# S1 of Strassen's scheme by accumulating transfers from DRAM instead of an addition on DVE

## The chip, the cores and the metric

The kernel runs on one core of a Trainium2 chip. The metric is the device time of one execution, in microseconds (us). The kernel before took 2231.31, 2233.18 and 2235.49 us in three runs, a median of 2233.18 us. The engines are called as in the profile: PE does matmuls (PEld is its loading of weights), DVE, ACT and POOL work on vectors, SP issues transfers. POOL's instruction stream can issue transfers too.

## The reference, cut to what matters

Two layers of a decoder trunk; x is 512 tokens by 1024 features, all in float32. A layer is a half-step feed-forward block, a mixer with three groups of attention heads, a cross-attention into 256 memory tokens, and a second half-step feed-forward block, each behind a layer norm. The change touches the feed-forward blocks, of which there are four in all:

```python
def swiglu(x, w_in, w_out):
    a, b = jnp.split(x @ w_in, 2, axis=-1)
    return (jax.nn.silu(a) * b) @ w_out

x = layer_norm(ALPHA * x + 0.5 * swiglu(x, ffn1_w_in[l], ffn1_w_out[l]), ln_g[l, 0], ln_b[l, 0])
```

`w_in` is 1024 x 5632 (the two halves a and b of 2816 columns each), `w_out` is 2816 x 1024. It also touches a small table of the mixer: the sliding-window attention adds a bias per head and distance, looked up in `rel_bias` (32 buckets, 8 heads).

## The kernel before, in words

**Precision.** Every float32 matrix product is done as three matmuls on rounded parts: a value is split into a high part H (a cast, on ACT) and a low part L = value - H (a subtraction, on DVE), and H·H, H·L and L·H are accumulated in PSUM (`mm3`, L201). `prep` (L256) splits a weight block that has landed in a buffer `raw` into `wH` (ACT) and `wL` (DVE). Each has four buffers, so that the preparation can run up to four blocks ahead of PE. The activations are held transposed and split as `xTH` and `xTL`.

**A feed-forward block** (`Ffn`, L522) has eleven pairs q of column blocks of 256, for a and for b. The first two pairs (q = 0 and 1, the plain part, with f = 0 to 3) are ordinary products. For q = 2 to 10 one round of Strassen's scheme (in Winograd's form) is used: the 1024 rows of the weights are halved (a1, a2 for the half a; b1, b2 for the half b), the 512 tokens too (B11 to B22), and seven products of 24 matmuls of 256 columns take the place of eight. The right-hand sides T1 to T4, sums of the quarters of x, are formed once for each block in `combine` (L279) from `xr` = H + L; two of these four additions run on POOL, two on DVE. The left-hand sides are formed for each q: S1 = b1 + b2, S2 = S1 - a1, S3 = a1 - b1, S4 = a2 - S2, all in float32 on DVE, 128 x 1024 elements each, each followed by its own split into wH and wL. S1 and S2 share one buffer `sw`; S3 is written over b1, S4 over a2. The order of the seven products of a round in the program (L688 to L734) is: a1·B11, S1·T1, S2·T2, then b2·T4 of the round before, a2·B21, S4·B22 of the round before, and S3·T3.

**Weights.** `load` (L560) brings a1 and b1 as two transfers of 512 KB into one `raw` buffer, a2 and b2 into another. There are three `raw` buffers, so a1, b1 of the next round go into the buffer that S4 (in a2's place) of the round before frees, and a2, b2 of the next round into the one that S3 (in b1's place) of this round frees. All transfers are issued by SP, in one order.

**What sets the order.** The program is written as straight code; a scheduler of the framework then orders the instructions of each engine by its own estimate of when their operands are ready, and every engine runs its instructions strictly in that order. A wait at the head of an engine's queue holds everything behind it. A rough clock in the kernel (L33) decides when side work (`tick`) is put in between.

**Side work in the first block.** `swa_bias` (L463) builds the bias table of the mixer during the first feed-forward block: for each of eight heads a matmul, a fill of a tile F by POOL, a copy by DVE, and two transfers over DRAM. F has one buffer of its own. The tag `scr` (four buffers) serves the Strassen rounds as u2 and u3, among other uses.

Of the kernel before, what the change touches and what calls it, by code (L numbers as in the profile page):

```python
# [7 lines left out]
F32 = mybir.dt.float32  # L8
F32R = mybir.dt.float32r
AF = mybir.ActivationFunctionType  # L10
ALU = mybir.AluOpType

P = 128
# [9 lines left out]
SWH = 8  # L23
# [4 lines left out]
NB = 32  # L28
# [114 lines left out]
class Net:  # L143
# [215 lines left out]
    def out_proj(self, nk, act, wsrc, scale, l, lni, nxt, tail=4, drain_at=0, done=None):  # L359
# [4 lines left out]
        for c in range(2):  # L364
# [9 lines left out]
            body = gr[:len(gr) - ntail]  # L374

            cut = drain_at if c == 0 and drain_at else len(body)
            for gi, (k0, n) in enumerate(body[:cut]):
                if c == 0 and gi == 0 and not drain_at:
# [84 lines left out]
    def swa_bias(self):  # L463
        nc, A, c = self.nc, self.A, self.const
        self.biasT = c.tile([P, SWH, 2 * P], F32, name="biasT")
        with self.tc.tile_pool(name="biasp", bufs=1) as bp, \
                self.tc.tile_pool(name="biasd", bufs=1, space=bass.MemoryType.DRAM) as dp:
            hot = bp.tile([NB, P], F32, name="hot")
            nc.sync.dma_start(hot, A["bucket_hot"])
            rb = bp.tile([NB, SWH], F32, name="rb")  # L470
            nc.sync.dma_start(rb, A["rel_bias"])
            for h in range(SWH):
                yield 4.0
                b = self.bank()
                nc.tensor.matmul(b[:, :P], rb[:, h:h + 1].broadcast_to([NB, P]), hot, start=True, stop=True)
                F = bp.tile([P, 383], F32, tag="F", name=self.nm("F"), bufs=1)
                nc.gpsimd.memset(F, -1e30)
                nc.vector.tensor_copy(F[:, P:2 * P], b[:, :P])
                d = dp.tile([P * 383], F32, tag="biasD", name=self.nm("biasD"), bufs=SWH)
                nc.sync.dma_start(d.rearrange("(p n) -> p n", n=383), F)  # L480
                nc.sync.dma_start(self.biasT[:, h],
                                  d[127:127 + P * 382].rearrange("(p n) -> p n", n=382)[:, :2 * P])
# [39 lines left out]
class Ffn:  # L522
# [17 lines left out]
    def open(self):  # L540
        n = self.net
        self.ctx, self.inner = ExitStack(), ExitStack()
        self.fp = self.ctx.enter_context(n.tc.tile_pool(name=n.nm("ffn"), bufs=1))
        self.h = {}
        self.ip = self.inner.enter_context(n.tc.tile_pool(name=n.nm("ffnin"), bufs=1))
        self.p1 = [self.ip.tile([P, S], F32, name=n.nm("p1")) for _ in range(2)]
        self.sw = self.ip.tile([P, 4, 256], F32, name=n.nm("sw"))
        self.T = [[self.ip.tile([P, 4, self.HT], F32R, name=n.nm("T")) for _ in range(2)] for _ in range(4)]

    def block(self, q, part, half):  # L550
# [101 lines left out]
    def body(self, nxt):  # L652
        n, nc = self.net, self.net.nc
        V, ACT = nc.vector, nc.scalar
        prev = None

        def rest(r):

            q, Y, b2 = r["q"], r["Y"], r["b2"]
            self.product(Y, b2, "T4", False)  # L660
            V.tensor_mul(self.hid(q, 0), self.hid(q, 0), self.pair(Y))

        def last(r):

            q, W, u2, u3 = r["q"], r["W"], r["u2"], r["u3"]
            self.product(W, r["s4"], "B22", False)
            V.tensor_add(u2, W, u2)
            ACT.activation(self.hid(q, 1), self.pair(u2), AF.Silu)
            V.tensor_mul(self.hid(q, 1), self.hid(q, 1), self.pair(u3))

        self.open()
        for f in range(2 * self.PLAIN):
            q = f // 2
            if f % 2 == 0:
                self.h[q] = self.two("h")
            h = self.h[q][:, f % 2]
            bs = []
            for part in range(2):
                if f < 2:
                    W, b = self.first[2 * f + part]  # L680
                    n.proj_T(b, W, 256, 512)
                else:
                    W, b = self.cols(f, part), n.bank()
                    n.proj_T(b, W, 0, S)
                bs.append(b)
            ACT.activation(h, bs[0], AF.Silu)
            V.tensor_mul(h, h, bs[1])
            if f == 0:  # L688
                self.combine()
        for q in range(self.PLAIN, self.Q):  # L690
            a1, b1 = self.load(q, 0)
            a2, b2 = self.load(q, 1)
            s = self.sw
            V.tensor_add(s, b1, b2)
            p1, X = self.p1[q % 2], n.bank()
            self.product(X, a1, "B11", True)
            ACT.copy(p1, X)
            W, Y = n.bank(), n.bank()
            self.product(W, s, "T1", True)
            V.tensor_sub(b1, a1, b1)  # L700
            V.tensor_sub(s, s, a1)
            self.product(Y, s, "T2", True)
            V.tensor_add(Y, Y, p1)
            u2 = n.scr()
            ACT.copy(u2, Y)
            if prev:
                rest(prev)
            def p2():
                self.product(X, a2, "B21", False)
                self.gate1(q, X)  # L710
                V.tensor_sub(a2, a2, s)

            if q < self.Q - 1:
                p2()
            if prev:
                last(prev)
            self.product(Y, b1, "T3", False)
            u3 = n.scr()
            ACT.copy(u3, Y)
            V.tensor_add(u3, W, u3)  # L720
            if q == self.Q - 1:
                p2()
            prev = dict(q=q, Y=Y, W=W, b2=b2, s4=a2, u2=u2, u3=u3)
        rest(prev)
        last(prev)
        self.inner.close()
        with n.tc.tile_pool(name=n.nm("ffnh"), bufs=1) as hp:
            hs = {}

            def wsrc(k0, k, c):  # L730
                if c == 0:
                    q = k0 // 2
                    hs[q] = hp.tile([P, 2, S], F32R, name=n.nm("hH")), self.two("hL", F32R)
                    n.split(*hs[q], self.h[q])  # L734
                return n.w_rows(self.tag, self.w_out, k0, k, c * 512, FT)

            n.out_proj(FT, lambda f, t: [m[:, f % 2, t * P:(t + 1) * P] for m in hs[f // 2]], wsrc, 0.5 / ALPHA,
                       self.l, self.lni, nxt)
        self.ctx.close()
        n.enter(nxt)  # L740
# [699 lines left out]
```

## Time and profile before

| | |
|---|---|
| median of three runs | 2233.18 us (2231.31 to 2235.49) |
| profiled execution: its time | 2240.78 us |
| its span (first to last instruction) | 2239.1 us |
| PE busy | 2200.4 us (98%) |
| DVE busy | 1483.4 us (66%) |
| ACT busy | 935.2 us (42%) |
| POOL busy | 202.8 us (9%) |
| moved by DMA | 235.84 MB, 105 GB/s in the mean |
| the 36 additions S1 on DVE | 44.1 us busy |

The profiled execution is 7.6 us longer than the median of the other three; differences are made against its own span. PE's share says little by itself: matmuls overlap each other in the pipeline, so PE counts as busy while its matmuls come at less than their best rate. What PE loses shows in the distance from one matmul's start to the next, and in the length of a round. The chain of waits names for each moment the engine or transfer that the end of the run hung on. Helpers record most operations on line L121, so operations are told apart by their tiles: `sw<-raw,raw` is S1, `sw<-sw,raw` S2, `raw<-raw` S3, `raw<-raw,sw` S4; `wL<-sw,wH` is the split of S1 or S2, `wL<-raw,wH` that of the other blocks.

### The profile page before, as it was taken

The page shows a single profiled execution, that of the slowest core. Times are in us where ns is not written, and L with a number is a line of the kernel's source. Part 1 is how long each engine was busy: PE and PEld are TensorE (multiplying, and loading weights), DVE is VectorE, ACT ScalarE, POOL GpSimd, SP SyncE. Part 2 cuts the span into 40 slices and gives each one's busy share as a digit, 9 for nine tenths or more (in the row PEclk, how much of TensorE's full clock was granted, in tenths as well). Part 3 has the DMA queues.
Part 4 walks back from the last instruction along what each step waited for, and adds up shares of the span by engine and source line. Part 5 has one row for each costly group of instructions (what it writes and reads, how often), then busy time and mean ns, then how long its engine had stood idle before and what let it go on. Part 6 is the DMA issues. An engine that isn't in the chain of part 4 may idle for free.

```text
span 2239.1 us, 33522 instructions
## 1 busy us (share of the span) xinstructions
PE 2200.4 (98%) x13952; PEld 1977.7 (88%) x13952; DVE 1483.4 (66%) x2052; ACT 935.2 (42%) x1405; POOL 202.8 (9%) x264
## 2 busy tenths in 40 slices
PE   9999999999999999999999999999999999999998
PEld 8999888888788899998889998888887888999987
DVE  5777735778565777784377776367775757777834
ACT  3444522457524244452134444124574343344611
POOL 2000001241010200000020000013400102000000
PEclk9999999999999999999999999999999999999999
DMA  6333323232422333333242324332233313323431
GB/s 207 111 108 114 129 97 105 69 95 81 127 95 75 113 97 112 113 130 108 85 151 95 101 88 142 103 101 74 81 110 110 113 55 103 125 83 106 152 102 47
DMA packets 199549, 235.84 MB, mean 105 GB/s; under 512 B 6331, under 2 KB 158171, under 8 KB 199397
## 3 DMA queue, kind: packets, MB, share of 16 engines
q1 hardware_dynamic: 199396, 233.70, 32.7%
q8 instruction: 109, 1.79, 0.3%
q14 instruction: 44, 0.35, 0.0%
HBM read 230.01 MB, written 3.67 MB: 104 GB/s over the span
## 4 chain that ended last, share of the span: by engine, by line
PE 67%; DVE 20%; DMA 6%; issue 3%; ACT 2%; POOL 1%; SPq 0%; DVEq 0%; ACTq 0%; POOLq 0%
PE ps L194 65%; DVE wL L121 7%; DMA raw<-in_ffn_w_in_dram 6%; DVE sw L121 3%; DVE raw L121 2%; PE ps L199 2%; ACT wH L121 1%; DVE x_nat L121 1%; DVE scr L121 1%; DVE h L121 1%; DVE st L121 1%; DVE xTL L121 1%; POOL mlrs L121 1%; DVE xr L121 1%; DVE T L121 0%
## 5 line engine op out<-in xcount | busy, mean ns | idle before, releaser
L121 DVE TENSOR_TENSOR wL<-raw,wH 128x1024 fp32r<-128x1024 f32 (+2 forms) x423 | 501.4, 1199 | 416.3 <-ACT wH L121 409.6
L121 ACT CAST wH<-raw 128x1024 fp32r<-128x1024 f32 (+2 forms) x423 | 435.2, 1046 | 680.9 <-PE ps L194 521.1
L194 PE MATMUL ps<-xTH,wH 128*128 128x256 f32 (+1 forms) x1712 | 523.6, 306 | 1.0 <-ACT sc L121 1.0
L194 PE MATMUL ps<-xTL,wH 128*128 128x256 f32 (+1 forms) x1712 | 521.6, 305 | 2.9 <-DVE xTL L121 2.9
L194 PE MATMUL ps<-xTH,wL 128*128 128x256 f32 (+1 forms) x1712 | 519.7, 305 | 1.0 <-DVE wL L121 1.0
L194 PE MATMUL ps<-T,wH 128*128 128x256 f32 x2304 | 424.0, 285 | 1.6 <-ACT wH L121 1.5
L194 PEld LDWEIGHTS ps<-T,wH 128*128 128x128 f32 x2304 | 359.7, 192 | 5.4 <-ACT wH L121 4.4
L194 PEld LDWEIGHTS ps<-xTL,wH 128*128 128x128 f32 x1712 | 327.7, 191 | 17.1 <-DVE xTL L121 5.3
L194 PEld LDWEIGHTS ps<-xTH,wL 128*128 128x128 f32 x1712 | 327.5, 191 | 15.8 <-DVE wL L121 2.3
L194 PEld LDWEIGHTS ps<-xTH,wH 128*128 128x128 f32 x1712 | 327.6, 192 | 13.9 <-ACT sc L121 1.2
L194 PE MATMUL ps<-T,wL 128*128 128x256 f32 x1152 | 327.3, 286 | 12.7 <-DVE wL L121 12.7
L194 PE MATMUL ps<-wH,hH 128*128 128x512 f32 x704 | 274.5, 390 | 0.0
L194 PE MATMUL ps<-wH,hL 128*128 128x512 f32 x704 | 274.4, 390 | 0.0
L194 PE MATMUL ps<-wL,hH 128*128 128x512 f32 x704 | 274.0, 389 | 0.0
L194 PEld LDWEIGHTS ps<-T,wL 128*128 128x128 f32 x1152 | 220.2, 192 | 17.4 <-DVE wL L121 16.9
L121 POOL TENSOR_TENSOR rs<-ve,mhalf 128x1 f32<-128x1 f32 x32 | 30.1, 940 | 1734.1 <-DVE ve L121 1731.9
L194 PEld LDWEIGHTS ps<-wH,hL 128*128 128x128 f32 x704 | 132.1, 188 | 28.7 <-DVE hL L121 1.3
L194 PEld LDWEIGHTS ps<-wL,hH 128*128 128x128 f32 x704 | 132.2, 188 | 27.3
L194 PEld LDWEIGHTS ps<-wH,hH 128*128 128x128 f32 x704 | 132.2, 188 | 26.9
L121 ACT CAST wH<-sw 128x1024 fp32r<-128x1024 f32 x72 | 75.8, 1053 | 139.4 <-DVE sw L121 139.4
L121 DVE TENSOR_TENSOR wL<-sw,wH 128x1024 fp32r<-128x1024 f32 x72 | 88.0, 1222 | 38.6 <-ACT wH L121 38.6
L121 ACT CAST xTH<-ps 128x512 fp32r<-128x512 f32 x64 | 34.9, 590 | 155.1 <-PE ps L199 154.6
(243 smaller groups left out, 2973.0 us busy)
## 6 DMA issues: line engine op xcount, KB each, us to landing
raw<-in_ffn_w_in_dram SPq DMA_DIRECT2D x147, 512.0 KB, 4.9
raw<-in_ffn_w_out_dram SPq DMA_DIRECT2D x40, 1024.0 KB, 5.2
raw<-in_ffn_w_in_dram SPq DMA_DIRECT2D x28, 1024.0 KB, 5.2
raw<-in_xattn_w_kv_dram SPq DMA_DIRECT2D x16, 1024.0 KB, 5.4
raw<-in_mix_w_in_dram SPq DMA_DIRECT2D x18, 512.0 KB, 4.9
raw<-in_mix_w_in_dram SPq DMA_DIRECT2D x8, 1024.0 KB, 5.3
raw<-in_mix_w_out_dram SPq DMA_DIRECT2D x16, 512.0 KB, 4.8
raw<-in_xattn_w_q_dram SPq DMA_DIRECT2D x8, 1024.0 KB, 5.2
```

Of the source, the lines that this page charges most:

```text
L121: return f(*a, **k)
L194: self.nc.tensor.matmul(out, l, r, start=start, stop=stop, **k)
L199: self.nc.tensor.transpose(out, i, ident)
```

## The change

`sw` gets two buffers instead of one, and S1 is no longer added by DVE. SP loads b1 a second time, into `sw`; then POOL issues two transfers that bring b2 a second time and add it in flight to what is in `sw`, 256 KB each (the halves k = 0, 1 and k = 2, 3). To make room for the second buffer, the tiles of `swa_bias` lose their own pool and take `scr` buffers instead: one is kept for the two small inputs while all eight heads are made, and F takes another for each head.

```diff
     def swa_bias(self):
-        with self.tc.tile_pool(name="biasp", bufs=1) as bp, \
-                self.tc.tile_pool(name="biasd", bufs=1, space=bass.MemoryType.DRAM) as dp:
-            hot = bp.tile([NB, P], F32, name="hot")
+        with self.tc.tile_pool(name="biasd", bufs=1, space=bass.MemoryType.DRAM) as dp:
+            keep = self.scr()
+            hot, rb = keep[:NB, :P], keep[:NB, P:P + SWH]
             nc.sync.dma_start(hot, A["bucket_hot"])
-            rb = bp.tile([NB, SWH], F32, name="rb")
             nc.sync.dma_start(rb, A["rel_bias"])
...
-                F = bp.tile([P, 383], F32, tag="F", name=self.nm("F"), bufs=1)
+                F = self.scr()[:, :383]
                 nc.gpsimd.memset(F, -1e30)
...
         self.p1 = [self.ip.tile([P, S], F32, name=n.nm("p1")) for _ in range(2)]
-        self.sw = self.ip.tile([P, 4, 256], F32, name=n.nm("sw"))
...
             a2, b2 = self.load(q, 1)
-            s = self.sw
-            V.tensor_add(s, b1, b2)
+            s = self.ip.tile([P, 4, 256], F32, tag="sw", name=n.nm("sw"), bufs=2)
+            nc.sync.dma_start(s, self.block(q, 1, 0))
+            for k in (0, 2):
+                nc.gpsimd.dma_start(s[:, k:k + 2], self.block(q, 1, 1)[:, k:k + 2], accum_op=ALU.add)
             p1, X = self.p1[q % 2], n.bank()
```

The scheduler puts other instructions in other places for it. **DVE, one steady round of the first block** (numbers tell buffers apart). Before, from the split of a1 on:

```order
L121 TENSOR_TENSOR wL_1731<-raw_1722,wH_1730 128x1024
L121 TENSOR_TENSOR scr_1376<-ps_1315,scr_1376 128x512
L121 TENSOR_TENSOR sw_291<-raw_1722,raw_1725 128x1024
L121 TENSOR_TENSOR h_1435<-h_1435,scr_1497 128x2x256
L121 TENSOR_TENSOR raw_1722<-raw_1722 128x1024
L121 TENSOR_TENSOR scr_1719<-ps_1537,scr_1719 128x512
L121 TENSOR_TENSOR wL_1762<-sw_291,wH_1761 128x1024
L121 TENSOR_TENSOR sw_291<-sw_291,raw_1722 128x1024
L121 TENSOR_TENSOR wL_1792<-sw_291,wH_1791 128x1024
L121 TENSOR_TENSOR wL_1823<-raw_1503,wH_1822 128x1024
L121 TENSOR_TENSOR wL_1852<-raw_1725,wH_1851 128x1024
L121 TENSOR_TENSOR wL_1883<-raw_1503,wH_1882 128x1024
```

The same round in the changed program:

```order
L121 TENSOR_TENSOR wL_1743<-raw_1731,wH_1742 128x1024
L121 TENSOR_TENSOR raw_1731<-raw_1731 128x1024
L121 TENSOR_TENSOR wL_1774<-sw_1737,wH_1773 128x1024
L121 TENSOR_TENSOR sw_1737<-sw_1737,raw_1731 128x1024
L121 TENSOR_TENSOR scr_1382<-ps_1321,scr_1382 128x512
L121 TENSOR_TENSOR wL_1804<-sw_1737,wH_1803 128x1024
L121 TENSOR_TENSOR h_1441<-h_1441,scr_1503 128x2x256
L121 TENSOR_TENSOR wL_1835<-raw_1509,wH_1834 128x1024
L121 TENSOR_TENSOR scr_1728<-ps_1546,scr_1728 128x512
L121 TENSOR_TENSOR wL_1864<-raw_1734,wH_1863 128x1024
L121 TENSOR_TENSOR raw_1734<-raw_1734,sw_1737 128x1024
L121 TENSOR_TENSOR wL_1895<-raw_1509,wH_1894 128x1024
```

S1 is gone, the instructions on 512 columns have moved behind S2, and S4 (`raw_1734<-raw_1734,sw_1737`) stands ahead of the split of the round before's S4 (the last row).

**SP, steady rounds of the changed program**: where `sw` is loaded (L692) among the `raw` transfers (L560).

```order
L692 DMA sw_1512<-in_ffn_w_in_dram 128x4x256
L560 DMA raw_1281<-in_ffn_w_in_dram 128x4x256
L560 DMA raw_1281<-in_ffn_w_in_dram 128x4x256
L560 DMA raw_1284<-in_ffn_w_in_dram 128x4x256
L560 DMA raw_1284<-in_ffn_w_in_dram 128x4x256
L692 DMA sw_1737<-in_ffn_w_in_dram 128x4x256
L560 DMA raw_1506<-in_ffn_w_in_dram 128x4x256
L560 DMA raw_1506<-in_ffn_w_in_dram 128x4x256
```

`sw_1512` belongs to the round of `raw_1506`: it is issued one round ahead of that round's `raw` transfers, as soon as S4 of the round two before has read the buffer.

**POOL at the entry of the second feed-forward block.** In the changed program:

```order
L121 TENSOR_TENSOR wL_7416<-raw_7413,wH_7415 128x512 [waits DMAHW4_49,PE_49,Activation_49]
L121 DMA sw_7717<-in_ffn_w_in_dram 128x2x256 [waits DMAHW0_49,PE_49]
L121 DMA sw_7717<-in_ffn_w_in_dram 128x2x256
L121 DMA sw_7882<-in_ffn_w_in_dram 128x2x256 [waits DMAHW1_49,DMASW7_49,DMASW6_49]
L121 DMA sw_7882<-in_ffn_w_in_dram 128x2x256
L121 TENSOR_TENSOR xr_7512<-xTH_7114,xTL_7115 128x1024
L121 TENSOR_TENSOR xr_7518<-xTH_7114,xTL_7115 128x1024
```

Before, the two additions `xr` followed the split directly. Now the accumulating transfers of the first two Strassen rounds stand between, and the first of them waits for the load of `sw` to land. The entries of the third and fourth blocks read the same; in the first block the two additions are still ahead of the transfers. SP issues the two loads of `sw` there behind the third `raw` transfer of the plain part.

## The prediction

> **What bounds the kernel now.** I read the page first, then the chain of waits, then the Strassen rounds by themselves.
>
> ```profile
> span 2239.1 us, 33522 instructions
> PE 2200.4 (98%) x13952; PEld 1977.7 (88%) x13952; DVE 1483.4 (66%) x2052; ACT 935.2 (42%) x1405; POOL 202.8 (9%) x264
> PE 67%; DVE 20%; DMA 6%; issue 3%; ACT 2%; POOL 1%; SPq 0%; DVEq 0%; ACTq 0%; POOLq 0%
> ```
>
> PE is busy 98% of the span, yet a quarter of the chain that ended last runs over DVE and DMA. So in some stage PE is busy without running at its rate. The view of stretches, over six Strassen rounds of each block (from one addition S1 to the sixth after it), and PE's start times:
>
> ```profile
> 96.80:224.30 127.50, 124.06 (x1013) 121.94 (x1012) 96.07 (x97) 59.53 (x73) 0.00 (x0) 1.00 0.31 100
> sum 510.50, PE 497.66 PEld 490.79 DVE 384.07 ACT 237.44 POOL 0.00; mean PE 124.41 PEld 122.70 DVE 96.02 ACT 59.36 POOL 0.00
> ...
> 792.14 0.28 PE L194 MATMUL ps<-xTH,wH 128*128 128x256 f32 x1
> ...
> 792.50 0.40 PE L194 MATMUL ps<-xTH,wH 128*128 128x512 f32 x1
> ```
>
> The 24 rounds take 510.5 us, 21.27 each. Undisturbed, a matmul of 256 columns starts 0.12 us after the last (three steps lie between 792.14 and 792.50), and a round has 7 x 24 = 168: 20.16 us. So PE loses 1.11 us a round, 40 us over the 36 rounds of the kernel: all that relief of DVE can bring there. The chain of waits through one round says where:
>
> ```profile
> 130.91 1.12 DVE raw L121
> ...
> 133.19 0.37 SPq L562
> 133.60 5.25 DMA raw<-in_ffn_w_in_dram
> 138.97 1.23 DVE sw L121
> 140.20 0.60 DVE scr L121
> 140.80 1.13 DVE raw L121
> 141.93 0.67 DVE h L121
> 142.60 1.13 DVE wL L121
> 144.33 1.14 DVE sw L121
> ...
> 154.16 0.37 SPq L562
> ```
>
> This is a loop. The split of S3 ends at 133.2 and frees b1's buffer; SP loads the next a2, b2 into it; S1 on DVE waits for b2 until 138.97; behind it all of DVE's round follows in order, to the split of the next S3, which ends at 154.15. The loop is 20.98 us long, more than PE's 20.16. PE never runs dry for long, but each round waits for the loop.
>
> **The change, part by part.** *S1 leaves DVE* (in the groups of instructions):
>
> ```profile
> L121 DVE TENSOR_TENSOR sw<-raw,raw 128x1024 f32<-128x1024 f32 x36 | 44.1, 1225 | 49.6 <-DMA raw<-in_ffn_w_in_dram 49.4
> ```
>
> 44.1 us of work and 49.4 us of waiting go, but DVE has a fifth of its time idle; what counts is the loop. Without S1, a2 is first used by its own split, and the changed order puts that 8.1 us behind the split of a1 (the sum of S3 1.13, split of S1 1.14, S2 1.14, an addition 0.60, 0.57 of waiting for ACT, split of S2 1.14, h 0.67, split of b2 1.14, an addition 0.60; the waiting is from the row of 146.64 below). In this round that is 136.81 + 8.1 = 144.9, against data at 133.60 + 5.25 = 138.85: 6 us to spare. What is late next is a1:
>
> ```profile
> 126.81 3.49 DVE L121 TENSOR_TENSOR wL<-raw,wH 128x1024 fp32r<-128x1024 f32 x3
> 134.49 1.05 ACT L121 CAST wH<-raw 128x1024 fp32r<-128x1024 f32 x1 [2.96 <-DMA raw<-in_ffn_w_in_dram]
> 135.58 1.23 DVE L121 TENSOR_TENSOR wL<-raw,wH 128x1024 fp32r<-128x1024 f32 x1 [1.82 <-ACT wH L121]
> 146.64 1.23 DVE L121 TENSOR_TENSOR wL<-sw,wH 128x1024 fp32r<-128x1024 f32 x1 [1.17 <-ACT wH L121]
> ...
> 770.00:776.00 6.00, 6.00 (x54) 6.00 (x53) 5.96 (x12) 3.14 (x5) 3.87 (x4) 1.00 1.04 342
> ```
>
> The split of S4 ends at 130.30 and frees a1's buffer; a1 lands about 134.4, its own split ends at 136.81: 6.51 us. From there to the next split of S4 the changed order has S3 1.13, split of S1 1.14, S2 1.14, an addition 0.60, the rest of the 1.17 us in which ACT rounds S2 (0.57), split 1.14, h 0.67, split 1.14, addition 0.60, split 1.14, S4 1.12, split 1.14: 11.53. The loop is 18.04 us. *The load of sw* stands just ahead of a1 on SP, released by S4 one DVE step (1.14 us) earlier. It delays a1 by nothing or by its own transfer: 512 KB at 342 GB/s, what a stretch full of transfers moves (last row), are 1.5 us. So 18.0 to 19.5 us, and PE's 20.16 becomes the bound. I keep nine tenths of the 40, **-36 us**, since landings scatter.
>
> *The accumulating transfers* have no counterpart in this trace. Per 256 KB, from below: nothing beyond SP's 0.37 us of issue. From above, a transfer of that size to its landing, 5.6 us (in the issues by size, the last figure):
>
> ```profile
> raw<-in_ffn_w_in_dram SPq DMA_DIRECT2D x147, 512.0 KB, 4.9
> ...
> scr<-in_ln_b_dram SPq DMA_DIRECT2D x16, 256.0 KB, 5.6
> ```
>
> In steady rounds that is hidden: `sw` is loaded after S4 of round q and used by the split of S1 in round q+2, 40.3 us less the 9 us from that split to S4, so 31 us later; load and two halves in a row take 4.9 + 2 x 5.6 = 16 us. Cost nothing; without that cover, each us beyond 31 costs half a us a round.
>
> [...]
>
> *The entry of blocks 2 to 4* is where POOL's queue matters. POOL's first addition xr now stands behind four accumulating transfers, which wait for `sw`.
>
> ```profile
> 787.97 1.22 DVE xr L121
> 798.86 1.15 DVE wL L121
> ...
> 799.30:800.00 0.70, 0.19 (x1) 0.00 (x0) 0.70 (x2) 0.00 (x0) 0.00 (x0) 1.00 0.00 0
> ...
> GB/s 0 0 0 139 376 328 378 371 357 304 311 370 302 376 355 184 53 14 0 16 0 0 0 8 0 0 71 314 388 276 0 0 0 0 0 0 148 251 376 385
> ...
> GB/s 0 0 0 0 29 236 387 358 130 356 384 325 329 354 232 42 87 370 382 210 0 0 0 0 0 0 0 0 17 250 385 387 26 0 0 0 0 0 43 309
> ...
> GB/s 0 0 0 19 253 382 353 370 353 346 294 358 354 332 359 332 70 35 0 0 0 0 0 0 0 16 35 273 386 348 6 0 0 0 0 0 95 272 343 371
> ...
> 794.79 0.39 PE L194 MATMUL ps<-xTL,wH 128*128 128x512 f32 x1
> 795.70 0.39 PE L194 MATMUL ps<-xTH,wL 128*128 128x512 f32 x1
> ...
> 19.67 4.73 POOL L121 TENSOR_TENSOR xr<-xTH,xTL 128x1024 f32<-128x1024 f32 x2
> ...
> 1150.28 0.40 PE L194 MATMUL ps<-xTH,wH 128*128 128x512 f32 x1
> 1903.10 0.40 PE L194 MATMUL ps<-xTH,wH 128*128 128x512 f32 x1
> ```
>
> The rows of GB/s are forty slices of 1 us each, from 765, 1120 and 1875. In block 2 the data of the raw transfers end about 782.3. The two loads of sw follow at some 350 GB/s and land about 783.8 and 785.2. With a price c for POOL per accumulating issue, its first xr (4.73 / 2 = 2.4 us) ends at 783.8 + 4c + 2.4. DVE needs it for xr - xr; from there to the split of f = 3's first block is 12.0 us (787.97 to 800.01), the same eleven instructions as now. PE wants that split 48 matmuls after 792.50, at 0.2275 us each (0.91 us in four): 803.4. So POOL may be ready at 791.4, which c = 1.3 just meets. In blocks 3 and 4 PE starts there at 1150.28 and 1903.10, and data end about 1139.6 and 1891.3; that allows c = 1.4 and 1.7. Beyond, each us of c costs 4 us in each of three entries: 12c - 17.7 in all. c lies between 0.37 (SP's issue) and about 4.9 (POOL held until a transfer lands). I take 2, nearer to an issue than to a landing: **+6 us**. The changed order also moves the split of f = 2's second block ahead, which closes the 0.7 us in which PE starts nothing (one matmul's tail is left in the row of 799.30): **-2 us** for three entries.
>
> *The bias table* in block 1 moves into `scr`:
>
> ```profile
> POOL F L121 <- DMA biasD<-F: 52.1, 6, 24.7
> ```
>
> POOL's fill of F already waits for transfers. Now it also queues behind accumulating transfers that wait for S4, DVE's copy of F waits in order behind it, and u2, u3 wait for F's transfers. From nothing (the table is used only in the mixer) to eight heads times a wait of about 1 us: I take **+3 us**, once.
>
> **Sum:** -36 + 6 - 2 + 3 = -29, 2239.1 to 2210 us of span. The profiled execution (2240.78) lies 7.6 above the median of the runs, so **2204 us** in those terms.
>
> **The rivals.**
> (A) The forecast. c = 1 gives 2198, c = 3 gives 2216; range 2193 to 2222.
> (B) Slower: POOL is held until its transfer has landed. c = 4.9 makes the three entries cost 41 us in place of 6: 2239. It outweighs the gain from c = 4.4 on. For it: the second issue could need what the first holds; against it: SP is free after 0.37 us.
> (C) The accumulation itself is slow. Loop: buffer freed, load, two halves, split of S1, S4, 9 us, for two rounds: (4.9 + 9 + A) / 2 passes 21.27 from A = 28.6 us on. A = 35 gives 24.5 us a round: 2350. Against it: transfers of that size land in 5 to 6 us.
> (D) DVE slows while POOL issues. Rows:
>
> ```profile
> L121 DVE TENSOR_TENSOR xr<-xr,xr 128x1024 f32<-128x1024 f32 x16 | 19.5, 1218 | 0.0
> L121 DVE TENSOR_TENSOR xr<-xTH,xTL 128x1024 f32<-128x1024 f32 x8 | 16.9, 2148 | 0.0
> ```
>
> DVE's additions xr take 2148 ns beside POOL's, 1218 alone. At c = 2, 4 us a round at that pace cost 1.7 us: a loop of 19.7 to 21.2, so 2204 to 2240. [...]
> (E) No gain: a1 lands 3 us later beside 1 MB more traffic per round. The loop reaches 21.0, the gain shrinks to some 8 us and the entries eat it: 2232. Against it: these stretches show a DMA share of 0.31.
>
> **How the numbers follow.** Chances: A 0.60, B 0.15, C 0.06, D 0.08, E 0.11. What a measurement can tell here is about 0.2%, 4.5 us. Faster: A, most of D (0.05), a little of E (0.03): 0.68. Same: E 0.06, B 0.03, D 0.02: 0.11. Slower: B 0.12, C, the rest of D and E: 0.21. The range 2190 to 2240 takes in A, E, D and B to its upper bound, and leaves out C and A's lower tail; the lower end is a full 40 us with nothing paid.
>
> **What would show it.** Rounds of 20.2 us in the stretches; no S1 group and no DVE wait on b2; in the chain PE in place of DVE and DMA within rounds; ACT's wait for a1 no longer than now; `wH<-sw` never waiting for the accumulating transfers. Wrong, if rounds stay near 21, if PE has gaps of several us near the plain part of blocks 2 to 4 with DVE waiting for POOL's xr, or if DVE's 1218 ns grow.

## The result

The changed kernel takes 2260.93 us in the median of four runs (2257.25 to 2261.62), the kernel before on the same chip 2234.32 us (four runs). The ratio is 1.0111, with a 95% interval of 1.0099 to 1.0124: **slower by 1.1%, some 25 us**. 2204 us had been forecast, with a range up to 2240; the likeliest case has the wrong sign. Rival B, which had 0.15, is the one that came, and it came harder than its 2239 us. One run of the kernel with 1152 bytes, below, took 4359.94 us and is left out of its median.

The page of the changed kernel:

```profile
span 2259.9 us, 33859 instructions
PE 2199.5 (97%) x13952; PEld 1980.9 (88%) x13952; DVE 1449.6 (64%) x2016; ACT 928.7 (41%) x1405; POOL 287.4 (13%) x336
PE 83%; DVE 8%; issue 4%; POOL 2%; DMA 1%; ACT 1%; SPq 0%; DVEq 0%; POOLq 0%; ACTq 0%
...
raw<-in_ffn_w_in_dram SPq DMA_DIRECT2D x147, 512.0 KB, 6.2
...
sw<-in_ffn_w_in_dram POOLq DMA_DIRECT2D x72, 256.0 KB, 4.6
```

The chain that ended last now runs over PE for 83% of the span instead of 67%, and over DVE and DMA for 9% instead of 26%. The accumulating transfers land 4.6 us after their issue, and the raw transfers after 6.2 us instead of 4.9. By the chain alone the change did what it should, and yet the span is 20.8 us longer. (The profiled execution of the kernel before, 2240.78 us, lies 6.5 us above the median of its runs, that of the changed kernel 0.7; so the two profiles differ by less than the 25 us.)

**Where the time went.** PE executes the same number of matmuls between the same landmarks in both kernels, so the span can be cut into pieces with equal work: an *entry* of each feed-forward block (from the layer norm, its first `rs<-ve` on POOL, to PE's first product on T; for block 1 from the start), the *rounds* (from the first to the last matmul on T), and the rest. The view of stretches gives their lengths. The kernel before, the sums over four entries and over four blocks of rounds:

```profile
sum 263.95, PE 256.85 PEld 229.65 DVE 199.02 ACT 96.23 POOL 60.63; mean PE 64.21 PEld 57.41 DVE 49.76 ACT 24.06 POOL 15.16
...
sum 732.13, PE 717.87 PEld 708.58 DVE 547.70 ACT 344.50 POOL 1.68; mean PE 179.47 PEld 177.14 DVE 136.92 ACT 86.13 POOL 0.42
```

The changed kernel, the four entries with their sum, and the rounds of block 2 with the sum of all four blocks (the third figure from the right is the granted clock):

```profile
0.00:64.20 64.20, 60.71 (x370) 54.62 (x371) 37.91 (x47) 25.50 (x31) 19.69 (x29) 1.00 0.80 229
746.07:826.38 80.31, 69.08 (x409) 60.91 (x407) 52.46 (x65) 23.86 (x29) 19.44 (x14) 0.91 0.46 131
1110.74:1192.76 82.02, 68.53 (x407) 60.51 (x407) 53.10 (x66) 22.55 (x28) 19.41 (x14) 0.92 0.45 129
1869.87:1953.46 83.59, 69.59 (x408) 61.20 (x407) 53.55 (x66) 23.86 (x29) 19.54 (x14) 0.92 0.45 126
sum 310.12, PE 267.91 PEld 237.24 DVE 197.03 ACT 95.77 POOL 78.07; mean PE 66.98 PEld 59.31 DVE 49.26 ACT 23.94 POOL 19.52
...
826.38:1001.94 175.56, 175.56 (x1466) 175.56 (x1465) 129.54 (x128) 85.44 (x105) 17.00 (x14) 1.00 0.56 153
...
sum 706.99, PE 705.95 PEld 704.13 DVE 516.22 ACT 339.56 POOL 69.22; mean PE 176.49 PEld 176.03 DVE 129.05 ACT 84.89 POOL 17.31
```

The rounds gained 732.1 - 707.0 = 25.1 us. In blocks 2 to 4 they last 175.56 us each, with PE busy in all of it: that is PE's floor. The entries lost 310.1 - 264.0 = 46.2 us, 44.9 of it in blocks 2 to 4. The difference, 21.0 us, is the 20.8 of the spans; the rest of the program is the same within 0.5 us.

What the rounds gained hangs on the execution that they are compared with. The run with the bias table alone, below, does the same work in its rounds as the kernel before, and its span is 2235.1 us. Its four blocks of rounds:

```profile
sum 728.51, PE 716.71 PEld 707.29 DVE 548.46 ACT 346.76 POOL 1.26; mean PE 179.18 PEld 176.82 DVE 137.11 ACT 86.69 POOL 0.32
```

Its entries take 264.0 us, as before. Against that execution the rounds gained 21.5 us, the entries lost 46.1, and the span grew by 24.8, as the medians did.

**What happens at an entry.** POOL, DVE and PE of the changed kernel in block 2 (start, duration, engine, line, instruction; in brackets the idle time before and what ended it), then stretches of 5 us with the clock:

```profile
779.43 1.30 POOL L121 DMA_DIRECT2D sw<-in_ffn_w_in_dram  x1 [9.25 <-PE ps L194]
784.15 1.22 POOL L121 DMA_DIRECT2D sw<-in_ffn_w_in_dram  x1 [3.43 <-issue]
790.53 1.21 POOL L121 DMA_DIRECT2D sw<-in_ffn_w_in_dram  x1 [5.16 <-issue]
795.11 1.21 POOL L121 DMA_DIRECT2D sw<-in_ffn_w_in_dram  x1 [3.37 <-issue]
795.86 5.12 POOL L121 TENSOR_TENSOR xr<-xTH,xTL 128x1024 f32<-128x1024 f32 x2
...
798.73 3.35 DVE L121 TENSOR_TENSOR xr<-xr,xr 128x1024 f32<-128x1024 f32 x1 [14.70 <-POOL xr L121]
...
803.26 0.79 PE L194 MATMUL ps<-xTH,wL 128*128 128x512 f32 x1 [9.81 <-DVE wL L121]
...
811.68 3.48 DVE L121 TENSOR_TENSOR wL<-raw,wH 128x1024 fp32r<-128x1024 f32 x3
...
812.94 0.50 PE L194 MATMUL ps<-xTH,wL 128*128 128x512 f32 x1 [1.06 <-DVE wL L121]
...
800.00:805.00 5.00, 1.74 (x4) 1.45 (x5) 5.00 (x4) 2.16 (x3) 0.98 (x1) 0.50 0.08 24
805.00:810.00 5.00, 5.00 (x14) 3.85 (x14) 5.00 (x6) 3.50 (x5) 0.00 (x0) 0.55 0.54 186
810.00:815.00 5.00, 3.94 (x18) 2.94 (x17) 5.00 (x6) 2.35 (x3) 0.00 (x0) 1.00 0.16 40
```

An issue itself takes POOL 1.2 us. But the second starts 4.72 us after the first, the third 6.38 after that, the fourth 4.58 later. The transfers of the first three land at 783.83, 790.21 and 794.79 by the trace; each next issue starts 0.32 us after that, whatever it waited for. Nothing holds the addition xr behind the fourth: it begins 0.75 us after it. So the four keep POOL from xr for 16.43 us, 4.1 for each, where 2 had been taken; in blocks 3 and 4 it is 17.07 and 17.17 us. The addition begins 49.8 us after the start of the entry instead of 24.1, DVE sits 14.70 us waiting for it, and PE 9.81 us for the split that DVE makes behind it.

After the stall PE runs at 0.50 to 0.55 of its clock until about 809: its matmuls of 512 columns start 0.43 us apart instead of 0.2275. In this block that costs nothing. DVE goes through ten instructions without a pause from 798.73 to 811.68, and PE has to wait for the split that comes then, until 812.94, however fast it was before. Over the three entries PE's first stalls are 10.2, 11.9 and 11.9 us from start to start, the second ones 1.4, 2.0 and 2.6. Only in block 4 the half clock comes back after the second stall, and there the way from that stall to the first product on T takes 15.1 us instead of 13.4.

In all three blocks the long stall is followed by half clock, for 6.1, 4.9 and 3.6 us. It also followed much shorter stalls: behind the second one of block 4, of 2.6 us, stand seven steps of 0.43 us, and in block 4 of the run without the addition, below, a stall of 2.27 us has seven such steps behind it (0.98 of the clock granted in that entry). What sets these lengths is not shown by the runs.

### The profile page after: what moved, and what is told of

Its sections match the earlier page's. It is cut to its first block, busy times and chain, and to the rows that moved or that the text cites. A ratio compares the mean times of both kernels' runs of the same rounds, so it can differ in the third digit from the quotient of the medians.

```text
span 2259.9 us, 33859 instructions
## 1 busy us (share of the span) xinstructions
PE 2199.5 (97%) x13952; PEld 1980.9 (88%) x13952; DVE 1449.6 (64%) x2016; ACT 928.7 (41%) x1405; POOL 287.4 (13%) x336
## 4 chain that ended last, share of the span: by engine, by line
PE 83%; DVE 8%; issue 4%; POOL 2%; DMA 1%; ACT 1%; SPq 0%; DVEq 0%; POOLq 0%; ACTq 0%
PE ps L194 81%; DVE wL L121 2%; PE ps L199 2%; DVE x_nat L121 1%; DVE xTL L121 1%; DVE st L121 1%; DMA sw<-in_ffn_w_in_dram 1%; POOL mlrs L121 1%; POOL sw L121 1%; DVE xr L121 0%; DVE T L121 0%; POOL xr L121 0%; DVE Cb L121 0%; DMA x_nat<-in_x_dram 0%; DMA raw<-in_ffn_w_in_dram 0%
## 5 line engine op out<-in xcount | busy, mean ns | idle before, releaser
L121 ACT CAST wH<-raw 128x1024 fp32r<-128x1024 f32 (+2 forms) x423 | 439.9, 1044 | 767.7 <-PE ps L194 572.7
L194 PE MATMUL ps<-xTH,wL 128*128 128x256 f32 (+1 forms) x1712 | 525.1, 307 | 38.1 <-DVE wL L121 38.1
L194 PE MATMUL ps<-T,wH 128*128 128x256 f32 x2304 | 418.6, 283 | 0.0
L121 POOL DMA_DIRECT2D sw<-in_ffn_w_in_dram x72 | 87.7, 1219 | 627.0 <-issue 245.9
L121 DVE TENSOR_TENSOR wL<-sw,wH 128x1024 fp32r<-128x1024 f32 x72 | 87.9, 1221 | 22.6 <-ACT wH L121 22.5
```

The lines of the kernel that those rows point to most:

```text
L121: return f(*a, **k)
L194: self.nc.tensor.matmul(out, l, r, start=start, stop=stop, **k)
```

## The experiments

Two theories were first set against each other. Theory R: POOL cannot issue a second accumulating transfer while the first fills the room set by `dynamic_dma_scratch_size` (1024 bytes in both kernels; before the change POOL issued no transfer). That descriptors are what fills it is the author's reading; the runs vary its size alone. Theory S: POOL starts one such transfer only when the last has landed, whatever the room.

**More room.** Nothing else changes and no instruction moves.

```diff
-dynamic_dma_scratch_size=1024
+dynamic_dma_scratch_size=1152
```

> The changed kernel, with the memory that POOL's transfer descriptors get raised from 1024 to 1152 bytes a partition (the 128 bytes that are free); no instruction moves. Theory R (room): in the changed kernel each accumulating issue at an entry starts 0.32 us after the transfer before it has landed, because the descriptors of one fill the room; if one transfer needs a little over half of 1024 bytes, 1152 holds two, the second issue of a pair follows the first after about 1.2 us, and the entries of blocks 2 to 4 lose some 10 of their 10 to 12 us stalls less: about 2235. If it needs clearly more than half, nothing changes. Theory S (one at a time): POOL starts an accumulating transfer only when the last has landed, whatever room there is: 2261 as the changed kernel.

For 3072 bytes, the bias table gives up two of its eight heads:

```diff
-dynamic_dma_scratch_size=1024
+dynamic_dma_scratch_size=3072
-        self.biasT = c.tile([P, SWH, 2 * P], F32, name="biasT")
+        self.biasT = c.tile([P, 6, 2 * P], F32, name="biasT")    # and h % 6 for h where it is used
```

> The changed kernel with 3072 bytes of descriptor room; the 2 KB for it come from the bias table, which holds six heads in place of eight, so that the bias of two heads is wrong (no instruction is left out or moved). Theory R: all four issues of an entry follow each other in 1.2 us once sw has landed, POOL's xr is ready about 11 us earlier, PE's gaps of 10.2, 11.9 and 11.9 us close and the slow clock behind them with it: 2261 - 45 to 52 = 2209 to 2216. Theory S: 2261, issues still 4 to 6 us apart.

Measured: with 1152 bytes 2242.70 us against 2236.7 before (ratio 1.0017, 1.0001 to 1.0032), where about 2235 had been expected; with 3072 bytes 2233.94 (ratio 0.9986, 0.9974 to 0.9997). POOL at the entry of block 2, first with 1152 bytes, then with 3072:

```profile
778.63 2.56 POOL L121 DMA_DIRECT2D sw<-in_ffn_w_in_dram  x2 [9.89 <-DMA sw<-in_ffn_w_in_dram]
784.15 1.21 POOL L121 DMA_DIRECT2D sw<-in_ffn_w_in_dram  x1 [2.96 <-issue]
788.14 1.21 POOL L121 DMA_DIRECT2D sw<-in_ffn_w_in_dram  x1 [2.78 <-issue]
788.90 5.16 POOL L121 TENSOR_TENSOR xr<-xTH,xTL 128x1024 f32<-128x1024 f32 x2
```

```profile
781.26 5.00 POOL L121 DMA_DIRECT2D sw<-in_ffn_w_in_dram  x4 [9.41 <-DMA sw<-in_ffn_w_in_dram]
784.32 6.72 POOL L121 TENSOR_TENSOR xr<-xTH,xTL 128x1024 f32<-128x1024 f32 x2
```

128 bytes more and two issues follow each other in 2.56 us, the third still waits; with 3072 all four go in 5.00 us. Theory R holds and S falls. By these rows the room holds one transfer at 1024 bytes, two at 1152 and at least four at 3072. But the time is not the 2209 to 2216 that R forecast: the entries fall only from 310.1 to 288.2 and 284.2 us, against 264.0 before. The rounds were already at the floor. So the room is 25.9 of the 46.2 us, and 20.2 remained. (The profiled execution with 1152 bytes took 2237.82 us, 4.9 less than the median of its runs.)

**The additions xr all on DVE**, so that nothing waits behind POOL's issues, with 1024 bytes:

```diff
-        for e, x in ((G, "B11"), (V, "B12"), (V, "B22"), (G, "B21")):
+        for e, x in ((V, "B11"), (V, "B12"), (V, "B22"), (V, "B21")):
```

> The changed kernel with all four additions xr on DVE, so that nothing at the entry waits behind POOL's accumulating transfers; they still go one at a time. If the wait of DVE for POOL's xr is the whole loss of the entries (52 us in three by the shift of the layer norms and of the first rounds), less two additions of 1.2 us on DVE three or four times: about 2212. If the accumulating transfers themselves (landing late, or taking the queue from the raw transfers) hold the entries too: 2225 to 2245.

Measured: 2237.09 us (ratio 0.9997, 0.9985 to 1.0008), entries 287.4 us. That is within the second expectation, if one lets the transfers hold something besides POOL. In block 2 ACT now waits at its head for a plain transfer of the raw weights (`wH<-raw`, 2.84 us of idle time) that was issued at 789.36, among the accumulating ones, and PE has two stalls of 2.0 and 3.0 us there. Blocks 3 and 4 have the same two stalls (1.8 and 3.0, 2.7 and 3.0 us). That these transfers slowed each other is argued; the next two runs take the parts away one at a time, with xr back on POOL.

**Without the addition, and without POOL's transfers.** The first, with 3072 bytes, overwrites b1 by b2; the second leaves sw at b1:

```diff
-                nc.gpsimd.dma_start(s[:, k:k + 2], self.block(q, 1, 1)[:, k:k + 2], accum_op=ALU.add)
+                nc.gpsimd.dma_start(s[:, k:k + 2], self.block(q, 1, 1)[:, k:k + 2])
```

> The kernel with 3072 bytes of descriptor room, its POOL transfers without the addition: they overwrite b1 by b2, so S1 is b2 (and the bias of two heads is wrong as there). Same bytes from DRAM, same order. With 3072 bytes and the addition the entries still cost 20 us (4.4, 5.7, 4.1, 6.0), and the plain part's raw transfers land after 7 us instead of 5. Theory A (the addition in flight is what slows the transfers): they land faster, the entries cost less than 10 us, total about 2222. Theory B (it is the bytes and the queue): 2234 again.

```diff
-            for k in (0, 2):
-                nc.gpsimd.dma_start(s[:, k:k + 2], self.block(q, 1, 1)[:, k:k + 2], accum_op=ALU.add)
```

> The changed kernel without POOL's transfers: sw holds b1 alone, so S1 is b1; SP's second load of b1 stays. If POOL's queue and its transfers are the loss at the entries, all of it goes and the rounds stay at 175.6 us a block: 2239 - 25 = 2214 in the frame of the profiled execution, 2208 to 2212 in that of the medians. If SP's extra load ahead of the raw loads is a part of the loss, 1.5 us for each load of 512 KB, two at each of four entries: 12 us more, 2222.

Measured: 2218.63 us (ratio 0.9917, 0.9902 to 0.9932) and 2211.58 us (0.9888, 0.9874 to 0.9901), against 2237.12 before in the same set of runs. Their entries:

```profile
sum 271.22, PE 258.12 PEld 230.31 DVE 205.47 ACT 95.87 POOL 69.91; mean PE 64.53 PEld 57.58 DVE 51.37 ACT 23.97 POOL 17.48
```

```profile
sum 262.04, PE 257.50 PEld 230.27 DVE 201.61 ACT 96.23 POOL 62.93; mean PE 64.37 PEld 57.57 DVE 50.40 ACT 24.06 POOL 15.73
```

So of the loss at the entries, in this order of steps: 25.9 us were the room, 284.2 - 271.2 = **13.0 us the addition in flight**, 271.2 - 262.0 = **9.2 us POOL's transfers as such**. By the ratios of the runs the three steps are about 28, 15 and 6.5 us (the first with 1.4 us of the rounds in it), so each size is good to 2 or 3 us. SP's second load of b1 costs nothing (262.0 against 264.0). Theory A holds: the entries cost 7.3 us more than before, under its 10, and B's 2234 is not what came.

What the addition does there is seen on POOL and DVE. In block 2, with 3072 bytes, first with the addition (its four issues are in the row of 781.26 above), then without it:

```profile
782.75 1.22 DVE L121 TENSOR_TENSOR xr<-xTH,xTL 128x1024 f32<-128x1024 f32 x1
...
784.32 4.38 POOL L121 TENSOR_TENSOR xr<-xTH,xTL 128x1024 f32<-128x1024 f32 x1
...
784.48 7.65 DVE L121 TENSOR_TENSOR xr<-xTH,xTL 128x1024 f32<-128x1024 f32 x1
...
L121 POOL DMA_DIRECT2D sw<-in_ffn_w_in_dram x72 | 88.4, 1569 | 551.4 <-DMA sw<-in_ffn_w_in_dram 276.7
sw<-in_ffn_w_in_dram POOLq DMA_DIRECT2D x72, 256.0 KB, 8.8
```

```profile
778.49 2.98 POOL L121 DMA_DIRECT2D sw<-in_ffn_w_in_dram  x4 [9.31 <-DMA sw<-in_ffn_w_in_dram]
781.49 4.77 POOL L121 TENSOR_TENSOR xr<-xTH,xTL 128x1024 f32<-128x1024 f32 x2
...
781.49 2.42 POOL L121 TENSOR_TENSOR xr<-xTH,xTL 128x1024 f32<-128x1024 f32 x1
...
781.81 5.53 DVE L121 TENSOR_TENSOR xr<-xTH,xTL 128x1024 f32<-128x1024 f32 x1
...
L121 POOL DMA_DIRECT2D sw<-in_ffn_w_in_dram x72 | 52.4, 730 | 569.0 <-ACT scr L121 269.5
sw<-in_ffn_w_in_dram POOLq DMA_DIRECT2D x72, 256.0 KB, 6.3
```

The four issues are done at 781.26 + 5.00 = 786.26 us with the addition, 1.2 us for each, and at 778.49 + 2.98 = 781.47 without it, 0.7 for each; over all 72, POOL is busy for 88.4 and 52.4 us. POOL's addition xr looks nearly twice as long with it, 4.38 us instead of 2.42. But its record begins while the fourth issue is still running, and from 786.26 to its end at 788.70 are 2.44 us: by these records POOL adds as fast as without, and begins later. DVE's addition (7.65 and 5.53 us) begins beside POOL's two and ends 1.1 us after the second of them in both runs, 792.13 after 791.04 and 787.34 after 786.26. Beside POOL's issues alone DVE's earlier addition takes its usual 1.22 us (782.75).

So at an entry the addition in flight costs 0.5 us of POOL for each issue, 2 us for four. DVE's chain of xr and T ends that much later, and so does PE's stall: 56.4 us after the start of the entry instead of 54.3. The rest is the clock. The stall is 3.96 us long instead of 1.84, a dozen steps at half clock follow it and none the shorter one (0.95 of the clock granted in this entry against 1.00), and PE does not wait again, so that block 2's entry takes 72.5 us instead of 67.8. The transfers land later too, after 8.8 us instead of 6.3 in the median, but no wait on that path names them.

**Nothing at the entry.** S1 of the first two rounds of each block stays on DVE (1024 bytes); then that of the first round alone, with 1152 bytes, and the same with 1024:

```diff
+            if q < self.PLAIN + 2:          # or + 1
+                V.tensor_add(s, b1, b2)
+            else:
                 nc.sync.dma_start(s, self.block(q, 1, 0))
                 ...
```

> The changed kernel (1024 bytes of descriptor room), but S1 of the first two Strassen rounds of each block stays on DVE; loads of sw and accumulating transfers begin with the third, so none lies at an entry. Theory E (all the loss is at the entries: in the changed kernel 46 us from the layer norms to PE's first product on T, against 25 us gained in the rounds): the entries return to what they were before and the rounds keep most of the 25: 20 us below the kernel before, about 2214 to 2218. Theory L (the accumulating transfers cost something in the rounds too): the rounds' stretches are longer than 175.6 us or other stretches longer, and the time is within 8 us of the kernel before.

> The same with S1 of the first Strassen round alone on DVE and 1152 bytes of descriptor room, so that one sw load and one pair of accumulating transfers remain at each entry, which POOL can issue without waiting between them. Theory E: between the run before it and the kernel with 1152 bytes: an entry pays the time in which one pair holds back the raw loads and POOL, some 1 to 3 us each: 2218 to 2226. If even one pair costs a whole PE stall with its slow clock: 2230 or more.

> The kernel with S1 of the first round on DVE, with 1024 bytes of descriptor room instead of 1152. POOL's additions xr now stand ahead of the accumulating transfers in blocks 2 to 4, so the room should matter there little (66.5, 67.7, 66.7 us as with 1152). In the first block POOL's fills of F stand between the transfers, DVE's copy of F waits in order behind them: with 1024 the second issue of a pair again waits for the first to land, and block 1 should lose 3 to 8 us as in the run with two rounds on DVE (186.0 us of rounds against 180.0): 2217 to 2222. If room does not matter in that block: 2214.

| | us, median | ratio to before (95%) | entries | rounds, block 1 | rounds, blocks 2 to 4 |
|---|---|---|---|---|---|
| first two on DVE, 1024 | 2220.09 | 0.9928 (0.9915 to 0.9940) | 264.9 | 186.0 | 3 x 175.6 |
| first one on DVE, 1152 | **2214.26** | **0.9901 (0.9888 to 0.9915)** | 263.1 | 180.0 | 3 x 175.6 |
| first one on DVE, 1024 | 2219.77 | 0.9919 (0.9903 to 0.9936) | 264.0 | 186.2 | 176.1, 175.6, 175.6 |

Theory E holds: with no accumulating transfer ahead of POOL's xr the entries are what they were before, and the rounds keep their gain. One round on DVE is enough: the transfers of the next round then come after xr in POOL's order, at 805 us in block 2 of the run with 1152 bytes. With the same room of 1024 bytes one and two rounds on DVE cost the same (0.9919 and 0.9928). The first of the three runs misses its 2214 to 2218 by 2 us, with block 1 at 186.0 us; the second lies 4 us below its 2218 to 2226, since the pair of transfers that was to cost 1 to 3 us an entry costs nothing there. The room shows almost only in block 1, for 6 us, as the last expectation had it. There POOL's fills of F stand between the transfers. From the run with two rounds on DVE, POOL, DVE and PE:

```profile
82.41 1.35 POOL L121 DMA_DIRECT2D sw<-in_ffn_w_in_dram  x1 [2.00 <-DMA sw<-in_ffn_w_in_dram]
87.88 1.23 POOL L121 DMA_DIRECT2D sw<-in_ffn_w_in_dram  x1 [4.12 <-issue]
88.61 0.93 POOL L121 MEMSET scr<- 128x383 f32 x1
...
89.57 0.29 DVE L121 COPY scr<-ps 128x128 f32<-128x128 f32 x1 [5.27 <-POOL scr L121]
...
91.05 0.58 PE L194 MATMUL ps<-T,wL 128*128 128x256 f32 x1 [3.56 <-DVE wL L121]
```

POOL waits 4.12 us before its second issue (in the run with the first round on DVE and 1152 bytes the first three pairs of block 1 go together, in 2.44 to 2.61 us), its fill of F stands behind, DVE's copy waits 5.27 us for the fill with three splits behind it, and PE runs dry for 3.56 us. **The kernel with the first round on DVE and 1152 bytes beats the kernel before by 1.0%** (some 22 us) and the changed one by 2%, and is 2.7 us from the run that has no transfer of POOL at all.

**The bias table alone**, in the kernel before:

```diff
-                F = bp.tile([P, 383], F32, tag="F", name=self.nm("F"), bufs=1)
+                F = self.scr()[:, :383]      # and hot, rb in one scr buffer
```

> The kernel before with only the second part of the change: the bias table's tiles in scr buffers, S1 still added on DVE, one sw buffer, no accumulating transfer. My forecast's term: +3 us (2237). Rival: the cost comes only with the accumulating transfers that POOL's fills queue behind; alone it changes nothing: 2234 within 2.

Measured: 2235.05 us (ratio 0.9992, 0.9980 to 1.0005): the rival's "nothing". It costs only with accumulating transfers in POOL's queue.

**One sw buffer** (first round on DVE, 1152 bytes):

```diff
-            s = self.ip.tile([P, 4, 256], F32, tag="sw", name=n.nm("sw"), bufs=2)
+            s = self.ip.tile([P, 4, 256], F32, tag="sw", name=n.nm("sw"), bufs=1)
```

> The kernel with S1 of the first round on DVE and 1152 bytes, with one sw buffer in place of two: the load of sw for a round starts only when S4 of the round before has read it. Theory (the forecast's cover of 31 us is the second buffer): the round becomes a loop of S4 to load 3.5 us, issue and the two accumulating transfers about 8 to 9 us, rounding and the 9 us from the split of S1 to S4: 21.5 to 22.5 us in place of 20.16, 7 rounds a block: 40 to 65 us more than with two buffers, 2254 to 2280. If the accumulating transfers are quick enough behind the load: rounds stay at 175.6 us a block and 2214.

Measured: 2400.3 us (ratio 1.0731, 1.0712 to 1.0749), far above the 2254 to 2280 expected; rounds of about 25.2 us in blocks 2 to 4 and 28 in block 1. The chain of waits through one round shows the loop:

```profile
1348.95 1.24 DVE raw L121
...
1350.25 3.50 DMA sw<-in_ffn_w_in_dram
...
1354.43 0.74 POOL sw L121
1355.17 9.30 DMA sw<-in_ffn_w_in_dram
...
1364.64 1.05 ACT wH L121
...
1365.72 1.24 DVE wL L121
```

From S4 to the end of the next split of S1 are 18.0 us, of which 13.5 are the load, the issue and the two accumulating transfers. From there to the next S4 (1374.13 in the trace) are 7.2 more, 25.2 in all. The expected loop was there, and longer than the 21.5 to 22.5 us: the issue and those transfers take 0.74 + 9.30 us, not 8 to 9. The clock is lower too (0.92 to 0.94 granted in the rounds of blocks 2 to 4); whether that lengthens the loop, and why block 1's rounds are longer still, stays open. Two buffers hide all of it: 175.56 us of rounds in each of blocks 2 to 4.

**S1 on POOL** from the raw buffers (two sw buffers, no extra transfer):

```diff
-            nc.sync.dma_start(s, self.block(q, 1, 0))
-            for k in (0, 2):
-                nc.gpsimd.dma_start(s[:, k:k + 2], self.block(q, 1, 1)[:, k:k + 2], accum_op=ALU.add)
+            nc.gpsimd.tensor_add(s, b1, b2)
```

> The changed kernel's two sw buffers, but S1 = b1 + b2 added by POOL from the raw buffers: no second load, no accumulating transfer. Theory W (what S1 costs on DVE is its 1.2 us of work): DVE is relieved as by the change, rounds near 175.6 us a block, about 2212. Theory L (what costs is the loop through the landing of b2, with S1 in it wherever it is added): the loop keeps b2's 5.6 us and its S1 takes 2.4 to 4.4 us on POOL in place of 1.2 on DVE: rounds no shorter than before, 2234 or more.

Measured: 2289.57 us (ratio 1.0233, 1.0217 to 1.0250); rounds of 195.0, 193.8 and 192.1 us in blocks 2 to 4, against 180 to 184 before. What POOL waited for:

```profile
L121 POOL TENSOR_TENSOR sw<-raw,raw x36: 2383/2398/2406, 60.1 to 2132.0; 128x1024 f32<-128x1024 f32 x36
...
  DMA raw<-in_ffn_w_in_dram: 579.2, 30
```

Theory L: DVE is relieved of the same 44 us, and the kernel is slower. S1 takes 2.4 us on POOL, 1.2 more than on DVE, and the 27 rounds of blocks 2 to 4 are 1.3 us longer each. It is b2's place in the loop that counts, which the extra load takes away, and not DVE's work.

## Why the prediction failed, step by step

- *What bounds the kernel*: right. Each round hung on b2's landing; with S1 out of that loop the rounds run at PE's floor of 175.56 us, and S1 on POOL shows that relief of DVE alone, with S1 left in the loop, brings nothing. (In the rounds shown DVE is idle for a quarter of the time, 384.07 of 510.50 us being busy, and not for a fifth; nothing hangs on it.)
- *-36 us for the rounds*: right in kind, too large; it measured -25.1, and -21.5 against the execution with the bias table alone. The term that was too large is the 1.11 us a round multiplied by 36. It was measured over six rounds of each block, and those 24 rounds (24 x 1.11 = 26.6) hold nearly all that was there: 732.1 - 705.2 (the floor, from the runs without a stall in block 1 either) = 26.9 us. The rounds at the ends of a block lost next to nothing.
- *The accumulating transfers hidden in steady rounds*: right; one buffer shows what the cover is worth.
- *+6 us at the entries*: **this is the step that failed.** "I take 2, nearer to an issue than to a landing": counted as the formula counts it, from the first issue to the addition xr, c was 16.43 / 4 = 4.1, 4.3 and 4.3. The choice rested on SP's 0.37 us, and SP's queue is no near row for POOL's, whose four issues started 4.6 to 7.0 us apart with 1024 bytes of room and went in 5.00 us together with 3072. The code names that room, and the prediction did not ask how many transfers it holds. Rival B had the nearer end (4.9) for nearly the right reason ("the second issue could need what the first holds"): POOL is not held until each landing, since its addition follows the fourth issue at once, but the next issue is.
- *The formula for the entries* (12c - 17.7) gives 33 us with the measured c of 4.2; the entries of blocks 2 to 4 lost 44.9. Its two missing terms: the first issue came later after the start of the entry than the formula has it, by 0.8, 1.0 and 3.3 us, and DVE's first xr - xr, beside POOL's second addition, took 3.35 us instead of 1.22 each time, 6.4 in all. With these it is 44.5, and smaller terms of both signs are left.
- *-2 us for the gap of 0.7 us*: not seen in the changed kernel, where new stalls of 1.4 to 2.6 us stand there.
- *+3 us for the bias table*: 1.3 us in block 1's entry and 180.3 - 178.6 = 1.7 us in its rounds, together 3.0. That this is the fills' doing is argued for the changed kernel; the mechanism is shown in other kernels (5.27 us of DVE's waiting, 6 us of time), and alone it costs nothing.
- *Rival C*: the transfers land after 4.6 us each in the median, under the 5.6 that the prediction took from above, and far from 28.6 for the two. *Rival D*: DVE's instructions in the rounds take 1.22 us as before; only beside POOL's additions at the entries do they slow (3.35 us at 798.73, and 7.65 at 784.48 with 3072 bytes), and beside its issues alone they do not (1.22 us at 782.75 with 3072 bytes). *Rival E*: raw transfers of 512 KB do land later, 6.2 us instead of 4.9, and the loop had room for that.

## What to carry to other kernels

Here each accumulating transfer took 1.2 us of POOL's queue, and with 1024 bytes of room the next issue at an entry of blocks 2 to 4 started 4.6 to 7.0 us after it, with POOL's additions behind: before moving an addition into such transfers, ask how many of them the room holds and which of POOL's other instructions stand behind. The 128 bytes more were worth 22 us of 46 at the entries of the profiled executions. Leaving the first round of each block as it was turned a loss of 1.1% into a gain of 0.8%, and of 1.0% with those 128 bytes. When a cost is bounded from both sides and its two ends decide the sign, the choice needs a reason from the same queue, not from another engine's.

## What had not been expected of the hardware

- Accumulating in flight is not free for POOL: an issue of 256 KB keeps it busy for 1.2 us instead of 0.7. POOL's and DVE's own additions are not slower for it, they come later; with the stalls and the slow clock behind that, it is 13.0 us over four entries.
- A stall of PE can cost more than its length. With 3072 bytes, block 2's stall of 3.96 us is followed by a dozen matmuls of 512 columns 0.43 us apart where the steps before it are 0.2275 (0.83 of the clock granted from 800 to 820 us), and from its end to the first product on T it is 16.1 us; without the addition, where full clock follows a stall of 1.84 us, it is 13.5. Where PE has to wait again for DVE, as in blocks 2 and 3 of the changed kernel, the slow steps cost nothing.
- The clock granted over an entry went with PE's idle time there (the length of the stretch less PE's busy time). The stretches of the two kernels and of ten runs, all but the one with the bias table alone, hold 36 entries of blocks 2 to 4: in the 20 with at most 2.14 us of idle time it was 1.00, in the 14 with 2.76 us or more 0.91 to 0.98, and of the two between, 2.24 us had 0.98 and 2.73 us 1.00.
